# Strassen feed-forward stage: wider weight rings half a product later, combining of the sums spread over the last weight tiles

## The chip, the cores and the metric

The kernel runs on one core of a Trainium2 chip. The metric is device time in microseconds (us); the kernel before took 2602.29 us, the median of three runs (2601.42 to 2602.42). The profile is of one further execution of the same program.

## The reference, cut to what matters

One decoder layer on 512 tokens of width 2048, all in float32: a mixing half (two groups of recurrent heads, an output projection, norms), and then the feed-forward (FF) half, which is where the change lies:

```python
h = rmsnorm(x, pre_ffn_norm[l]) * (1.0 + sc_f) + sh_f
y = jnp.square(jax.nn.relu(h @ w_ff1[l])) @ w_ff2[l]      # 2048 -> 8192 -> 2048
x = x + gt_f * rmsnorm(y, post_ffn_norm[l])
```

## The kernel before

**Split products.** Each float32 matrix is split into a rounded part (H) and a remainder (L), and a product is three matmuls: H by H, L by H and H by L. For the weights this is done on the fly by `WeightStream`: SyncE (SP) loads a 128x1024 tile into `raw`, ScalarE (ACT) casts it to `wh` (line 197), VectorE (DVE) subtracts to get `wl` (line 199). I call this subtraction the split.

**The order of the weights** is a plan, a list of tiles numbered from 0, which `get` hands out one by one. With each `get` it also issues loads, casts and splits of some tiles further on. Tiles 168 to 171 are the first four of the FF stage, 504 and 505 the last two of the first FF matrix, 506 to 509 and 510 to 513 the eight after them.

**The rings.** `raw`, `wh` and `wl` are rings of 3, 2 and 2 buffers in the pool `wpool`, which lives through the whole kernel. In the FF stage `ws.wide` is set to the pool `fp`, and then every second `raw` and every third `wh`/`wl` comes from `fp` instead (tags `raw2`, `wh2`, `wl2`), so that the rings are twice and one and a half times as deep; `get` also works two tiles ahead instead of one. `fp` takes the memory that the stage in between (pool `mid`) had, so a tile of `fp` can only be written once the last instruction on `mid` is done.

**The stage in between** ends with 16 blocks of `h2`, the input of the FF stage: for each, TensorE (PE) transposes (line 1519), DVE scales (line 1525), ACT makes `h2H` (line 1528, or lines 1533 and 1534 for every third block), and DVE (line 1529) or, for every third block, GpSimd (POOL, line 1535) makes `h2L`. The last two blocks are number 14 (its `h2L` on POOL) and 15 (on DVE). The first FF product runs between these transposes.

**The FF stage.** The 8192 hidden units go in 16 rounds of 512. `ff1(r, g)` makes half a round: 4 weight tiles (q = 0 to 3), 24 matmuls each, 96 in all; tile q needs the `h2` blocks 4q to 4q+3. `ff2s(r, m)` multiplies into the second matrix by Strassen's seven products (84 matmuls), whose results DVE adds onto `y2` and, for products 4 and 5, onto `m45`. Only after the last of these can `gather` combine `m45` and the quarters of `y2`: 24 additions of 128x512 on DVE, line 1634. The last round is not by Strassen: its halves of the second matrix (`ff2_mm`, banks `pg`, at the end `pl`) are multiplied plainly. The order before the end is `ff2s(14, 1)`, `plain(0)`, `gather`, `ff1(15, 1)`, `plain(1)`, then the plain products. Two weight tiles of these (510 and 511) are written as `walt` into the memory of `m45`.

**What sets the order.** In the FF loop PE and SP run in the order in which the code calls them; on DVE, ACT and POOL a scheduler orders the instructions when the program is built. Behind that, each engine takes its instructions strictly in turn, and SP starts its transfers in turn.

Of the kernel before, what the change touches and what calls it, by code (L numbers as in the profile page):

```python
# [13 lines left out]
ALU = mybir.AluOpType  # L14
# [221 lines left out]
def hybrid_layer_kernel(  # L236
# [7 lines left out]
    nc = tc.nc  # L244
# [63 lines left out]
    def ff_order():  # L308

        yield from ((1, 0, 0), (1, 0, 1))  # L310
        for r in range(NR - 1):
            last = r == NR - 2
            yield from ((1, r + 1, 0), (2, r, 0))
            yield from ((2, r, 1), (1, r + 1, 1)) if last else ((1, r + 1, 1), (2, r, 1))
# [30 lines left out]
    ws = WeightStream(nc, wpool, plan, 3, 1, (3, 2, 2))  # L345
# [119 lines left out]
    def mm3(ps, aH, aL, bH, bL, start, stop):  # L465
        mm(ps, aH, bH, start, False)
        mm(ps, aH, bL, False, False)
        mm(ps, aL, bH, False, stop)
# [436 lines left out]
    def pj(name):  # L905
        return bank("pj", name)
# [538 lines left out]
    with ExitStack() as st:  # L1445
# [70 lines left out]
        for kt in range(KT):  # L1516
# [10 lines left out]
            if kt % 3 < 2:  # L1527
                nc.scalar.activation(out=h2H[:, kt, :], in_=ht, func=AF.Identity, bias=shf[:, kt : kt + 1])
                nc.vector.scalar_tensor_tensor(out=h2L[:, kt, :], in0=ht, scalar=shf[:, kt : kt + 1],
                                               in1=h2H[:, kt, :].bitcast(F32), op0=ALU.add, op1=ALU.subtract)  # L1530
            else:
# [4 lines left out]
                                        op=ALU.subtract)  # L1536
# [3 lines left out]
    with ExitStack() as st:  # L1540
        fp = st.enter_context(tc.tile_pool(name="ff", bufs=1))
        y2 = big.tile([P, 4, D], F32, tag="y", name="y2")
# [14 lines left out]

        m45 = fp.tile([P, 4, 1024], F32, tag="m45", name="m45")
        gs, cs_, gHL = {}, {}, []

        def ff1(r, g):
            if g == 0:
                gs[r] = fp.tile([P, 2, 2, T], F32, tag="g", name=f"g{r}")
            col = r * RB * P + g * 256
            pss_ = [pj(f"pf{col}_{cb}") for cb in range(2)]
            for q in range(4):
                wH, wL = ws.get(("f1", col, q))
                for cb in range(2):
                    for kk in range(4):
                        kt = q * 4 + kk  # L1570
                        cs = slice(cb * P, (cb + 1) * P)
                        mm3(pss_[cb], wH[:, kk, cs], wL[:, kk, cs], h2H[:, kt, :], h2L[:, kt, :],
                            kt == 0, kt == KT - 1)
            for cb in range(2):
                v = gs[r][:, cb, g, :]
                nc.scalar.activation(out=v, in_=pss_[cb], func=AF.Relu)
                nc.scalar.activation(out=v, in_=v, func=AF.Square)

        def combos(r):

            cH = fp.tile([P, 2, 7, 256], F32R, tag="cH", name=f"cH{r}")
            cL = fp.tile([P, 2, 7, 256], F32R, tag="cL", name=f"cL{r}")
            for jj in range(2):
                S = fp.tile([P, 5, 256], F32, tag="gS", name=f"gS{r}_{jj}")
                g4 = gs[r][:, jj].rearrange("p h (t n) -> p (h t) n", t=2)
                nc.vector.tensor_tensor(out=S[:, 0:2, :], in0=g4[:, 0:2, :], in1=g4[:, 2:4, :], op=ALU.add)
                nc.vector.tensor_tensor(out=S[:, 2:4, :], in0=g4[:, 1:3, :], in1=g4[:, 0::3, :], op=ALU.subtract)
                nc.vector.tensor_tensor(out=S[:, 4, :], in0=g4[:, 0, :], in1=g4[:, 3, :], op=ALU.add)
                nc.scalar.copy(out=cH[:, jj, 0:5, :], in_=S)
                nc.vector.tensor_tensor(out=cL[:, jj, 0:5, :], in0=S, in1=cH[:, jj, 0:5, :].bitcast(F32),  # L1590
                                        op=ALU.subtract)
                nc.scalar.copy(out=cH[:, jj, 5:7, :], in_=g4[:, 0::3, :])
                nc.vector.tensor_tensor(out=cL[:, jj, 5:7, :], in0=g4[:, 0::3, :],
                                        in1=cH[:, jj, 5:7, :].bitcast(F32), op=ALU.subtract)
            cs_[r] = (cH, cL)
# [13 lines left out]
        def ff2s(r, m):  # L1609
            cH, cL = cs_[r]  # L1610
            for i, *_ in SEVEN:
                wH, wL = ws.get(("s2", r, m, i))
                for tb in range(2):
                    ps = bank(RING[nps[0] % 5], f"pg{r}_{m}_{i}_{tb}")
                    nps[0] += 1
                    ts = slice(tb * P, (tb + 1) * P)
                    for jj in range(2):
                        mm3(ps, cH[:, jj, PLACE[i], ts], cL[:, jj, PLACE[i], ts], wH[:, jj, :], wL[:, jj, :],
                            jj == 0, jj == 1)
                    for dst, first in sums_of(i, m, tb):  # L1620
                        if r == 0 and first:
                            nc.vector.tensor_copy(out=dst, in_=ps)
                        else:
                            nc.vector.tensor_tensor(out=dst, in0=ps, in1=dst, op=ALU.add)  # L1624

        def gather(m):

            lo_, hi_ = slice(m * 512, (m + 1) * 512), slice(1024 + m * 512, 1024 + (m + 1) * 512)
            for tb in range(2):
                c11, c12, c21, c22 = y2[:, tb, lo_], y2[:, tb, hi_], y2[:, 2 + tb, lo_], y2[:, 2 + tb, hi_]  # L1630
                m4, m5 = m45[:, tb, lo_], m45[:, 2 + tb, lo_]
                for dst, v, op in ((c11, m4, ALU.add), (c11, m5, ALU.subtract), (c22, c12, ALU.add),
                                   (c22, c21, ALU.subtract), (c12, m5, ALU.add), (c21, m4, ALU.add)):
                    nc.vector.tensor_tensor(out=dst, in0=dst, in1=v, op=op)  # L1634

        def plain(g):

            r = NR - 1
            if g == 0:
                gHL.append(fp.tile([P, RB, T], F32R, tag="cH", name="gH"))  # L1640
                gHL.append(fp.tile([P, RB, T], F32R, tag="cL", name="gL"))
            for cb in range(2):
                j = 2 * g + cb
                nc.scalar.copy(out=gHL[0][:, j, :], in_=gs[r][:, cb, g, :])
                nc.vector.tensor_tensor(out=gHL[1][:, j, :], in0=gs[r][:, cb, g, :],
                                        in1=gHL[0][:, j, :].bitcast(F32), op=ALU.subtract)
# [26 lines left out]
                next(steps, None)  # L1673

        ws.on_get = on_get
        ws.wide = fp
        ws.nraw, ws.ring = 0, []
        with tc.manual_schedule(engines={ET.PE, ET.SP}):
            for kind, r, g in ff_order():
                if kind == 1:  # L1680
                    ff1(r, g)
                    if g == 1 and r == 0:
                        combos(0)
                    if r == NR - 1 and g == 1:
                        plain(1)
                else:
                    ff2s(r, g)
                    if g == 1 and r < NR - 2:
                        combos(r + 1)
                    elif g == 1:  # L1690
                        plain(0)
                        gather(0)
                        gather(1)
            for _ in steps:
                pass

# [99 lines left out]
```

## Time and profile before

| what | value |
|---|---|
| median of three runs | 2602.29 us |
| the profiled execution: its time, its span from first to last instruction | 2601.19 us, 2599.4 us |
| PE busy | 2476.1 us, 95% |
| DVE busy | 1876.1 us, 72% |
| ACT busy | 1119.0 us, 43% |
| POOL busy | 1034.3 us, 40% |
| chain that ended last: PE, DVE | 66%, 6% of the span |
| FF stage | from about 1245.6 us to the end |

PE is busy nearly all the time, so what counts are the places where it is not. These are found in the chain that ended last (which engine carried the time in each stretch), and then in the timeline of PE, where a bracket behind a row gives the idle time before it and what ended it. Times in such rows are from the start of the span.

### The profile page before, as it was taken

What the parts mean: (1) busy time and instruction counts of PE and PEld (TensorE: products, weight loads), DVE (VectorE), ACT (ScalarE), POOL (GpSimd) and SP (SyncE); (2) the same over time, 40 slices, a digit from 0 to 9 for tenths busy, and PEclk for the clock granted to TensorE, in tenths of its full rate; (3) what the DMA queues carried; (4) which work ended last, traced back from release to release, by engine and by line L of the source; (5) the groups of instructions that cost most, each with busy time, mean ns of one, the idle gap of its engine ahead of it and who ended that gap; (6) DMA issues with size and microseconds to landing.
All of it is one profiled execution on the core that took longest, in us unless ns stands there. A gap on an engine that the chain in (4) does not pass through costs nothing.

```text
span 2599.4 us, 34113 instructions
## 1 busy us (share of the span) xinstructions
PE 2476.1 (95%) x12627; PEld 2008.6 (77%) x12627; DVE 1876.1 (72%) x2709; ACT 1119.0 (43%) x1765; POOL 1034.3 (40%) x646
## 2 busy tenths in 40 slices
PE   5889999998999899999899999999999999999998
PEld 3667777777877788788688888888888888888876
DVE  7997877767676675634568776787767877677696
ACT  5543544444444442423444444444444444434333
POOL 5561344445454540000144535445354453533423
PEclk9999999999999999999899999999999999999999
DMA  9762434444544432435323333333324334233234
GB/s 324 253 196 78 131 120 139 139 155 139 156 151 142 154 107 90 140 128 170 122 98 135 101 134 105 134 131 105 134 97 142 130 100 140 85 122 109 89 113 160
DMA packets 127300, 350.64 MB, mean 135 GB/s; under 512 B 14247, under 2 KB 18713, under 8 KB 125981
## 3 DMA queue, kind: packets, MB, share of 16 engines
q1 hardware_dynamic: 126938, 348.41, 40.0%
q8 instruction: 99, 1.62, 0.3%
q14 instruction: 67, 0.55, 0.1%
q10 hardware_dynamic: 196, 0.06, 0.0%
HBM read 340.01 MB, written 8.40 MB: 134 GB/s over the span
## 4 chain that ended last, share of the span: by engine, by line
PE 66%; DVE 6%; POOL 1%; ACT 1%; issue 1%; DMA 1%; SPq 0%; DVEq 0%; ACTq 0%; POOLq 0%
PE pf L331 26%; PE pg L331 21%; PE pj L331 9%; PE pout L331 7%; DVE wl L199 1%; PE pa L331 1%; DMA ada<-in_w_ada_dram 1%; DVE y L1634 0%; POOL y L1720 0%; DVE y L1624 0%; DVE uc L1034 0%; POOL aacc L451 0%; DVE utmp L1032 0%; DVE x2r L1738 0%; PE p L331 0%
## 5 line engine op out<-in xcount | busy, mean ns | idle before, releaser
L199 DVE TENSOR_TENSOR wl<-raw,wh 128x1024 fp32r<-128x1024 f32 x506 | 723.9, 1432 | 441.8 <-ACT wh L197 438.5
L197 ACT CAST wh<-raw 128x1024 fp32r<-128x1024 f32 x512 | 538.2, 1052 | 946.3 <-PE pf L331 286.0
L165 POOL TENSOR_TENSOR raw<-raw,raw 128x1024 f32<-128x1024 f32 x150 | 439.9, 2948 | 401.6 <-DMA raw<-in_w_ff_dram 154.0
L331 PE MATMUL pf<-h2H,wh 128*128 128x512 f32 x1024 | 401.3, 392 | 6.6 <-ACT wh L197 6.6
L331 PE MATMUL pf<-h2H,wl 128*128 128x512 f32 x1024 | 401.1, 392 | 4.5 <-DVE wl L199 4.4
L331 PE MATMUL pf<-h2L,wh 128*128 128x512 f32 x1024 | 400.9, 391 | 0.0
L451 POOL TENSOR_TENSOR aacc<-ada,aacc 128x512 f32<-128x512 f32 x180 | 270.7, 1504 | 254.5 <-ACT ada L449 243.2
L331 PE MATMUL pg<-wl,cH 128*128 128x512 f32 x840 | 327.4, 390 | 1.1 <-DVE wl L199 1.0
L331 PE MATMUL pg<-wh,cL 128*128 128x512 f32 x840 | 326.8, 389 | 0.0
L331 PE MATMUL pg<-wh,cH 128*128 128x512 f32 x840 | 326.8, 389 | 0.0
L331 PE MATMUL pj<-hH,wh 128*128 128x512 f32 x768 | 325.3, 424 | 0.0
L331 PE MATMUL pj<-hH,wl 128*128 128x512 f32 x768 | 305.2, 397 | 4.3 <-DVE wl L199 4.3
L331 PE MATMUL pj<-hL,wh 128*128 128x512 f32 x768 | 304.0, 396 | 0.0
L331 PEld LDWEIGHTS pf<-h2H,wh 128*128 128x128 f32 x1024 | 193.7, 189 | 47.1 <-ACT wh L197 7.0
L331 PEld LDWEIGHTS pf<-h2H,wl 128*128 128x128 f32 x1024 | 193.5, 189 | 45.7 <-DVE wl L199 5.6
L331 PEld LDWEIGHTS pf<-h2L,wh 128*128 128x128 f32 x1024 | 193.6, 189 | 40.2
L451 POOL TENSOR_TENSOR gacc<-ada,gacc 128x512 f32<-128x512 f32 x64 | 108.5, 1695 | 277.9 <-ACT ada L449 277.9
L1624 DVE TENSOR_TENSOR y<-pg,y 128x512 f32<-128x512 f32 x344 | 218.9, 681 | 0.0
L331 PEld LDWEIGHTS pg<-wl,cH 128*128 128x128 f32 x840 | 157.6, 188 | 35.7 <-DVE wl L199 3.1
L331 PEld LDWEIGHTS pg<-wh,cH 128*128 128x128 f32 x840 | 157.7, 188 | 32.9
L331 PEld LDWEIGHTS pg<-wh,cL 128*128 128x128 f32 x840 | 157.7, 188 | 32.6
L331 PEld LDWEIGHTS pj<-hH,wl 128*128 128x128 f32 x768 | 146.5, 191 | 39.6 <-DVE wl L199 6.5
(434 smaller groups left out, 3762.2 us busy)
## 6 DMA issues: line engine op xcount, KB each, us to landing
raw<-in_w_ff_dram SPq DMA_DIRECT2D x256, 512.0 KB, 4.0
raw<-in_w_in_dram SPq DMA_DIRECT2D x128, 512.0 KB, 3.4
ada<-in_w_ada_dram SPq DMA_DIRECT2D x256, 256.0 KB, 3.5
adas<-in_w_ada_dram SPq DMA_DIRECT2D x128, 256.0 KB, 4.3
raw<-in_w_out_dram SPq DMA_DIRECT2D x40, 512.0 KB, 3.5
xo<-in_x_dram SPq DMA_DIRECT2D x8, 512.0 KB, 9.7
xr<-in_x_dram SPq DMA_DIRECT2D x8, 512.0 KB, 6.3
x2d<-z SPq DMA_DIRECT2D x4, 1024.0 KB, 3.9
```

The lines of the kernel that those rows point to most:

```text
L165: self.nc.gpsimd.tensor_tensor(out=out, in0=ra, in1=rb, op=op)
L197: self.cast = self.nc.scalar.copy(out=h, in_=raw).ins
L199: eng.tensor_tensor(out=lo, in0=raw, in1=h.bitcast(F32), op=ALU.subtract)
L331: nc.tensor.matmul(ps, lhsT=lhsT, rhs=rhs, start=start, stop=stop)
L451: nc.gpsimd.tensor_tensor(out=acc, in0=a, in1=acc, op=ALU.add)
L1624: nc.vector.tensor_tensor(out=dst, in0=ps, in1=dst, op=ALU.add)
```

## The change

Two edits, both in the FF stage.

First, `ws.wide = fp` (and the reset of the raw ring) is no longer set ahead of the FF loop but behind the first `ff1`, after four weight tiles. Tiles 168 to 171 thus stay in `wpool`'s rings of 3, 2 and 2, with `get` working one tile ahead for the split and three for the loads.

Second, `gather` becomes a generator that issues one addition per step and holds the additions in program order. It is no longer run in one piece before `ff1(15, 1)`: each of that function's four weight tiles takes five steps right behind its `get`, and what is left (four) comes behind `ff1(15, 1)`. The 24 additions are the same, on the same operands.

```diff
@@ ff1
                 wH, wL = ws.get(("f1", col, q))
+                for _ in range(5):
+                    next(joins, None)
                 for cb in range(2):
@@ gather
-        def gather(m):
...
-            for tb in range(2):
...
-                    nc.vector.tensor_tensor(out=dst, in0=dst, in1=v, op=op)
+        def gather():
+            for m in range(2):
...
+                for tb in range(2):
...
+                        tc.keep_in_program_order(nc.vector.tensor_tensor(out=dst, in0=dst, in1=v, op=op))
+                        yield
@@ the FF loop
         ws.on_get = on_get
-        ws.wide = fp
-        ws.nraw, ws.ring = 0, []
         with tc.manual_schedule(engines={ET.PE, ET.SP}):
             for kind, r, g in ff_order():
                 if kind == 1:
                     ff1(r, g)
+                    if (r, g) == (0, 0):
+
+                        ws.wide = fp
+                        ws.nraw, ws.ring = 0, []
                     if g == 1 and r == 0:
                         combos(0)
                     if r == NR - 1 and g == 1:
+                        for _ in joins:
+                            pass
                         plain(1)
                 else:
                     ff2s(r, g)
...
                     elif g == 1:
                         plain(0)
-                        gather(0)
-                        gather(1)
+                        joins = gather()
```

What stands on DVE at the start of the FF stage, where tiles 170 and 171 (the third and fourth of the first product) are split, before:

```order
L1525 SCALAR_TENSOR_TENSOR h2t14_11407<-pm14_11402,sc1f_102,R_10324 128x512
L1525 SCALAR_TENSOR_TENSOR h2t15_11418<-pm15_11413,sc1f_102,R_10324 128x512
L1529 SCALAR_TENSOR_TENSOR h2L_11272<-h2t15_11418,shf_103,h2H_11271 128x512
L199 TENSOR_TENSOR wl170_11441<-raw170_11052,wh170_11440 128x1024
L199 TENSOR_TENSOR wl172_11501<-raw1_11474,wh172_11500 128x1024
L199 TENSOR_TENSOR wl173_11531<-raw2_11504,wh173_11530 128x1024
```

and now:

```order
L1525 SCALAR_TENSOR_TENSOR h2t14_11407<-pm14_11402,sc1f_102,R_10324 128x512
L1525 SCALAR_TENSOR_TENSOR h2t15_11418<-pm15_11413,sc1f_102,R_10324 128x512
L199 TENSOR_TENSOR wl171_11499<-raw171_11436,wh171_11498 128x1024
L1529 SCALAR_TENSOR_TENSOR h2L_11272<-h2t15_11418,shf_103,h2H_11271 128x512
L199 TENSOR_TENSOR wl172_11529<-raw172_11466,wh172_11528 128x1024
L199 TENSOR_TENSOR wl174_11571<-raw174_11526,wh174_11570 128x1024
```

Before, the split of 170 stood behind the last `h2L`, and that of 171 twelve rows above it, between the scalings of blocks 9 and 10. Now 170 stands in that higher place and 171 just ahead of the last `h2L`.

The SP queue in the same place, before:

```order
L1468 DMA xr3_1_11247<-in_x_dram 128x1024
L1483 DMA x2d_10315<-z_10319 128x2048 x2
L140 DMA raw1_11474<-in_w_ff1_dram 128x1024
L140 DMA raw2_11504<-in_w_ff1_dram 128x1024
L140 DMA raw3_11534<-in_w_ff1_dram 128x1024
```

and now:

```order
L1468 DMA xr3_1_11247<-in_x_dram 128x1024
L1483 DMA x2d_10315<-z_10319 128x2048 x2
L140 DMA raw173_11496<-in_w_ff1_dram 128x1024
L140 DMA raw174_11526<-in_w_ff1_dram 128x1024
L1546 DMA gacc2_11429<-in_b_ada_dram 1x2048
L431 DMA ada5_0_0_11534<-in_w_ada_dram 128x512
L140 DMA raw0_11574<-in_w_ff1_dram 128x1024
L140 DMA raw1_11604<-in_w_ff1_dram 128x1024
```

`raw1` of before (tile 172) was the first tile of `fp` in this queue. Now tiles 173 and 174 go into `wpool`, 172 is loaded before the rows shown, and the first load into `fp` is `raw1` of now (tile 176).

DVE around the combining, before (the end of it, with the splits of tiles 504 to 507):

```order
L1634 TENSOR_TENSOR y2_11428<-y2_11428,m45_11430 128x512 x3
L1634 TENSOR_TENSOR y2_11428<-y2_11428 128x512
L199 TENSOR_TENSOR wl504_20630<-raw303_20517,wh504_20629 128x1024
L1634 TENSOR_TENSOR y2_11428<-y2_11428 128x512
L1634 TENSOR_TENSOR y2_11428<-y2_11428,m45_11430 128x512 x2
L199 TENSOR_TENSOR wl505_20660<-raw304_20633,wh505_20659 128x1024
L199 TENSOR_TENSOR wl506_20690<-raw305_20663,wh506_20689 128x1024
L199 TENSOR_TENSOR walt_20794<-raw309_20833,walt_20794 128x1024
L199 TENSOR_TENSOR wl507_20720<-raw306_20693,wh507_20719 128x1024
```

and now, from the last sum of Strassen's products on:

```order
L1627 TENSOR_TENSOR m45_11430<-pg14_1_5_1_20589,m45_11430 128x512
L1650 TENSOR_TENSOR gL_20598<-g15_20156,gH_20597 128x512 x2
L199 TENSOR_TENSOR wl504_20606<-raw299_20517,wh504_20605 128x1024
L1638 TENSOR_TENSOR y2_11428<-y2_11428,m45_11430 128x512 x2
L1638 TENSOR_TENSOR y2_11428<-y2_11428 128x512 x2
L1638 TENSOR_TENSOR y2_11428<-y2_11428,m45_11430 128x512
L199 TENSOR_TENSOR wl505_20641<-raw300_20609,wh505_20640 128x1024
L1638 TENSOR_TENSOR y2_11428<-y2_11428,m45_11430 128x512 x3
L1638 TENSOR_TENSOR y2_11428<-y2_11428 128x512 x2
L199 TENSOR_TENSOR wl506_20676<-raw301_20644,wh506_20675 128x1024
L1638 TENSOR_TENSOR y2_11428<-y2_11428,m45_11430 128x512 x4
L1638 TENSOR_TENSOR y2_11428<-y2_11428 128x512
```

The split of 504 stood behind 21 of the 24 additions (one of them stood earlier, amid the last Strassen products) and now stands ahead of all 24; then come five additions per split, and the `walt` splits have moved behind the splits of 507, 508 and 509.

## Rows read from the trace of the kernel before

**Rows 1.** The chain that ended last, merged: start us, us, what.

```profile
1272.27 55.40 PE pf L331 x238
1327.66 19.04 PE pg L331 x84
1346.70 21.76 PE pf L331 x96
```

**Rows 2.** Timeline of PE, start of the FF stage: start us, us, instruction.

```profile
1263.99 0.39 PE L331 MATMUL pf<-h2H,wl 128*128 128x512 f32 x1
1271.01 0.80 PE L331 MATMUL pf<-h2H,wh 128*128 128x512 f32 x1 [6.62 <-ACT wh L197]
...
1274.89 0.39 PE L331 MATMUL pf<-h2H,wl 128*128 128x512 f32 x1
```

**Rows 3.** Waits of the DMA queue SP, 1230 to 1330: total us, times, longest.

```profile
SPq L140 <- DVE h2L L1529: 29.3, 1, 29.3
```

**Rows 4.** Timeline of DVE, start of the FF stage.

```profile
1265.74 1.40 DVE L1525 SCALAR_TENSOR_TENSOR h2t<-pm,sc1f,R 128x512 f32<-128x512 f32 x2
1268.60 1.23 DVE L1529 SCALAR_TENSOR_TENSOR h2L<-h2t,shf,h2H 128x512 fp32r<-128x512 f32 x1 [1.47 <-ACT h2H L1528]
```

**Rows 5.** Timeline of ACT, start of the FF stage.

```profile
1256.73 1.06 ACT L197 CAST wh<-raw 128x1024 fp32r<-128x1024 f32 x1 [1.84 <-PE pf L331]
...
1263.32 1.38 ACT L1528 ACTIVATE h2H<-h2t,shf 128x512 fp32r<-128x512 f32 x2
1266.57 0.72 ACT L1533 ACTIVATE h2s<-h2t,shf 128x512 f32<-128x512 f32 x1 [1.88 <-DVE h2t L1525]
...
1269.91 1.04 ACT L197 CAST wh<-raw 128x1024 fp32r<-128x1024 f32 x1 [1.34 <-POOL h2L L1535]
```

**Rows 6.** Timeline of POOL, start of the FF stage.

```profile
1268.02 1.26 POOL L1535 TENSOR_TENSOR h2L<-h2s,h2H 128x512 fp32r<-128x512 f32 x1 [3.41 <-ACT h2H L1534]
```

**Rows 7.** Page, part 6, DMA issues: count, KB each, median us to landing.

```profile
raw<-in_w_ff_dram SPq DMA_DIRECT2D x256, 512.0 KB, 4.0
```

**Rows 8.** Timeline of PE, end of the FF stage.

```profile
2507.43 0.39 PE L331 MATMUL pg<-wh,cH 128*128 128x512 f32 x1
2507.92 0.50 PE L331 MATMUL pg<-wl,cH 128*128 128x512 f32 x1
...
2510.57 0.39 PE L331 MATMUL pf<-h2H,wh 128*128 128x512 f32 x1
...
2521.67 0.39 PE L331 MATMUL pf<-h2L,wh 128*128 128x512 f32 x1
2522.52 1.19 PE L331 MATMUL pg<-wh,gH 128*128 128x512 f32 x4 [0.46 <-ACT wh L197]
2528.16 0.80 PE L331 MATMUL pf<-h2H,wl 128*128 128x512 f32 x1 [4.45 <-DVE wl L199]
...
2541.36 0.39 PE L331 MATMUL pf<-h2H,wl 128*128 128x512 f32 x1
...
2564.74 0.62 PE L331 MATMUL pl<-walt,gH 128*128 128x512 f32 x2
```

**Rows 9.** Timeline of DVE, end of the FF stage.

```profile
2489.77 2.61 DVE L199 TENSOR_TENSOR wl<-raw,wh 128x1024 fp32r<-128x1024 f32 x1
...
2500.20 0.67 DVE L1634 TENSOR_TENSOR y<-y,m 128x512 f32<-128x512 f32 x1
...
2514.85 0.67 DVE L1634 TENSOR_TENSOR y<-y,m 128x512 f32<-128x512 f32 x1
...
2526.89 1.21 DVE L199 TENSOR_TENSOR wl<-raw,wh 128x1024 fp32r<-128x1024 f32 x1
```

**Rows 10.** Timeline of ACT, end of the FF stage.

```profile
2521.42 1.05 ACT L197 CAST wh<-raw 128x1024 fp32r<-128x1024 f32 x1 [4.38 <-PE pf L331]
```

**Rows 11.** Timeline of POOL, end of the FF stage.

```profile
2488.90 9.09 POOL L165 TENSOR_TENSOR raw<-raw,raw 128x1024 f32<-128x1024 f32 x3 [1.33 <-DMA raw<-in_w_ff_dram]
```

**Rows 12.** One window: us, then busy us (count) of PE, PEld, DVE, ACT, POOL; PEclk.

```profile
2500.00:2545.00 45.00, 39.99 (x161) 31.54 (x160) 38.22 (x53) 15.05 (x18) 0.00 (x0) 0.92 0.42 132
```

More of the change, by code (lines that the diff above doesn't have):

```diff
@@ L1559, in hybrid_layer_kernel @@
         gs, cs_, gHL = {}, {}, []
+        joins = iter(())
         def ff1(r, g):
@@ L1624, in ff2s @@
                             nc.vector.tensor_tensor(out=dst, in0=ps, in1=dst, op=ALU.add)
-        def gather(m):
-            lo_, hi_ = slice(m * 512, (m + 1) * 512), slice(1024 + m * 512, 1024 + (m + 1) * 512)
-            for tb in range(2):
[L1630 to L1633, printed above, removed]
-                    nc.vector.tensor_tensor(out=dst, in0=dst, in1=v, op=op)
+        def gather():
+            for m in range(2):
+                lo_, hi_ = slice(m * 512, (m + 1) * 512), slice(1024 + m * 512, 1024 + (m + 1) * 512)
+                for tb in range(2):
+                    c11, c12, c21, c22 = y2[:, tb, lo_], y2[:, tb, hi_], y2[:, 2 + tb, lo_], y2[:, 2 + tb, hi_]
+                    m4, m5 = m45[:, tb, lo_], m45[:, 2 + tb, lo_]
+                    for dst, v, op in ((c11, m4, ALU.add), (c11, m5, ALU.subtract), (c22, c12, ALU.add),
+                                       (c22, c21, ALU.subtract), (c12, m5, ALU.add), (c21, m4, ALU.add)):
+                        tc.keep_in_program_order(nc.vector.tensor_tensor(out=dst, in0=dst, in1=v, op=op))
+                        yield
         def plain(g):
```

## The prediction

> **What bounds the kernel now.** I read the chain that ended last first, in order of time. In the FF stage it lies on PE: 96 matmuls of a first-matrix product take 21.76 us and the 84 of a Strassen group 19.04 us [rows 1], 0.2267 us each, round after round. Nothing that spares DVE, ACT or DMA there is worth anything; only time in which PE doesn't run counts. The timeline of PE shows two such stretches, one at each end of the FF stage, and the edits lie on them. The reader is to see, in each, which instruction PE waits for, and what that one stood behind.
>
> At the start, PE is through the first two weight tiles with the matmul at 1263.99 and starts the third tile, 170, only at 1271.01, released by ACT's cast [rows 2]. That cast starts at 1269.91 [rows 5], right after the last h2L, which runs from 1268.60 for 1.23 us to 1269.83 [rows 4]. The data had been there: what held the cast is its buffer, the first of `fp`, which opens when `mid` is finished. SP's queue says the same: a weight load stood 29.3 us until that h2L [rows 3].
>
> At the end, PE runs through the last first-matrix product from 2510.57 [rows 8]. It multiplies with wh of tile 504 up to 2521.67, squeezes in 4 matmuls of the next product, and resumes at 2528.16, released by the split of 504. That split stands at 2526.89 [rows 9], behind 20 additions which began at 2514.85: (2526.89 - 2514.85)/20 = 0.60 us each.
>
> **The change part by part.**
>
> *A, the rings half a product later.* PE would go on at 1263.99 + 0.23 = 1264.22. It restarts at 1271.01: 6.79 us. Then the 8 matmuls before 1274.89 take 3.88 us [rows 2] where 8 x 0.2267 = 1.81 do at full clock: another 2.07 us at the lower of the two clock levels, 1.2 instead of 2.4 GHz, after that idle stretch. Together 8.86 us, if nothing else is late.
>
> What is late next? Tile 170 now takes the place that 171 had on ACT and DVE, and that one was cast at 1256.73 [rows 5], so with its split (1.2) it is ready by 1259.1. Tile 171 needs wh's second buffer, free when PE ends the second tile at about 1264.4. Its cast stands on ACT between the instruction that ends at 1263.32 + 1.38 = 1264.70 and the one at 1266.57, before which ACT sat idle 1.88 us for DVE [rows 5]. A cast of 1.06 fits, 1264.70 to 1265.76. Its split stands on DVE behind the two scalings that end at 1265.74 + 1.40 = 1267.14, and DVE then idled 1.47 us [rows 4], in which 1.21 fits. So neither delays h2. PE reaches tile 171 at 1264.22 + 24 x 0.2267 = 1269.66; it wants block 14 six matmuls later, at 1271.0, and block 15 at 1271.7. They are there by 1268.02 + 1.26 = 1269.28 [rows 6] and 1269.83.
>
> One rule speaks against this hiding. The last h2L took 1.23 us beside POOL's h2L of 1268.02, with 1.26 us [rows 4, 6]. The Trainium skill, "SBUF — State Buffer", section "Who interferes with whom", says that a VectorE instruction with two SBUF inputs and a GpSimd instruction that reads SBUF exclude each other, whichever comes second waiting for the whole of the other. By it the inserted split, until 1268.35, would hold POOL's h2L for 0.33 us and the last h2L until about 1270.4; the sum would stay as it is, and the chance that A loses a little is larger for it. The trace agrees in kind.
>
> The next product: 172 is loaded early now and takes the wh buffer of 170 at 1269.7, so it is ready by 1272.2, wanted at 1275.1. 174 waits for raw 171's buffer (1268.4), a transfer of 4.0 us [rows 7], cast and split: 1274.7. 173 takes the wh buffer of 171, free at 1275.3: ready at 1277.7, wanted at 1280.5. The loads of `fp` come behind `mid`'s end at 1269.83 for tiles wanted after 1290. So I take A at -8.86. The other end: the cast and split of 171 push the last h2L back by their whole 1.06 + 1.21 = 2.27 us, to 1272.1, where PE wants it at 1271.7; 0.4 us would go, and -8.4 be left. A longer wait there is among the rivals.
>
> *B, the additions spread.* From 2521.67 + 0.23 = 2521.90 to the last matmul of the product, 2541.36 + 0.23 = 2541.59, 19.69 us pass. In them run 96 - 50 = 46 matmuls of the product (50 lie between 2510.57 and 2521.67, (11.10/0.2267) + 1) and the 4 of the next [rows 8]: 50 x 0.2267 = 11.34. Lost: 8.35 us, again idle time and a stretch of matmuls at the lower clock behind it (the mean granted clock is 0.92 between 2500 and 2545 [rows 12]).
>
> Now the split of 504 stands ahead of all additions: where these began, at about 2514.3 to 2515.5, for a use at 2521.9. Then each weight tile brings five additions and one split, 5 x 0.60 + 1.21 = 4.2 us of DVE, beside 24 x 0.2267 = 5.44 us of PE. The cast of 506 comes at 2521.42, released by PE [rows 10]; its split ends by 2524 and is wanted at 2532. 507 is ready by 2529.2, wanted at 2537.7. The last four additions and the two gL splits end near 2536. So B is -8.35.
>
> *C, one addition less before.* One addition ran at 2500.20 [rows 9] amid the last Strassen group, where DVE had no gap, and PE loses 2507.92 - 2507.43 - 0.23 = 0.26 and some tenths about it [rows 8]. The addition gone, DVE is 0.60 us ahead. Between 0 and -0.6; I take -0.4.
>
> *D, what the additions hold.* The two casts of `walt` wait for the end of the additions, as m45 gives them its memory, and now stand on ACT among the casts of gacc2 behind the product, on which PE waits a little. Two casts are 2 x 1.06: cost between 0 and 2.1, below nothing not, since they leave no place that PE waited on. PE has the 20 matmuls of the next product ahead of that, 4.5 us, so I take +0.4. Their real use is the matmul at 2564.74 [rows 8], some 8 us earlier now, 2556; they are split by 2546.
>
> Both edits change no instruction count that matters: the same 24 additions, casts, splits and loads. The end behind the last product moves along with PE.
>
> Sum: -8.86 - 8.35 - 0.4 + 0.4 = -17.2. The profiled execution took 2601.19 us, its span 2599.4 and 1.8 around it; it would take 2584.0. The median of the runs stands 1.1 above it, so I predict 2602.29 - 17.2 = 2585.1.
>
> **The rivals.**
>
> *One half is lost.* Either h2 or a late tile holds PE at the start, or the additions hold the splits at the end. For the latter each DVE instruction would have to slow as one split did beside POOL's additions, 2.61 us against 1.21 [rows 9, 11]: +1.4 on six instructions is 8.4, so 12.6 against PE's 5.44 per tile, a new stall worth all of B. That is the rule named above, taken to the end. Against it: POOL is busy 0.00 us between 2500 and 2545 [rows 12]. With B gone the time is 2602.29 - 8.9 = 2593.4; with A gone, 2593.9; with half of either, about 2589 to 2590.
>
> *Neither comes.* PE's waits turn out to be followed by others of the same length, at h2 and at the tail, where DVE's and POOL's work behind the last matmul could set the end whenever PE is through. Against it: the additions and casts there stand in PE's order and move along. 2600 to 2603.
>
> *Slower: the phase of the rings.* The count that picks every third wh from `fp` now starts four tiles later, so each of the 15 Strassen rounds meets the ring one tile out of step with before. If one tile per round then came late by cast and split, 1.06 + 1.21 = 2.27 us, the price is 15 x 2.27 = 34 us, and the time 2602.3 + 34 - 17.2 = 2619. From 17.2/15 = 1.15 us per round on it decides. Against it: a round takes 22 tiles, no multiple of three, so before already ran through all phases, with the same 21.76 and 19.04 us.
>
> **How the numbers follow.** Both halves as worked out: 0.77, with its own range 2583 to 2588 (C and D at their ends, small losses of A). One half lost, wholly or partly: 0.13, 2589 to 2594. Neither: 0.05. Slower: 0.05. The range runs from 2581.5, for some waits of PE amid the last Strassen group that go too, to 2594. A measurement of this kernel tells about 0.2%, 5.2 us, from no change. Faster by more 0.90, within 0.05, slower by more 0.05.
>
> **What would show it.** A right: PE's row at 1271.01 loses its bracket, tile 170's matmuls start near 1264.2 at 0.39 us each, and the chain's PE stretch of 238 matmuls starts earlier by 8 to 9 us against the last transpose. B right: no PE idle time above 0.5 us between the last Strassen product and the first matmul on `walt`, granted clock 1.00 there, and the splits of 504 to 507 five additions apart. A wrong if PE waits behind 1264 for h2L or a split; B wrong if PE waits on line 199 in that product. The forecast as a whole is wrong if the rounds between are no longer 40.80 us.

## The result and the profile after

| | before | after |
|---|---|---|
| median of six runs | 2602.36 us (2601.42 to 2603.99) | 2585.27 us (2582.80 to 2589.01) |
| ratio, 95% interval | | 0.9934 [0.9921, 0.9947] |
| profiled execution, its span | 2601.19, 2599.4 us | 2583.66, 2581.9 us |

The change takes 17.1 us by the medians and 17.5 us by the two spans; 17.2 were forecast. To see where they went, the FF stage is cut at six matmuls of PE's timeline, each given by its start:

| us on PE | before | after | difference |
|---|---|---|---|
| last matmul of tile 169 | 1263.99 | 1264.31 | +0.32, drift ahead of the FF stage |
| from it to the first Strassen matmul | 63.51 | 54.63 | -8.88 |
| 28 pairs of a Strassen group and a product, 40.80 each | 1142.40 | 1142.40 | 0 |
| the last two Strassen groups, 168 matmuls with no product between them (to the last first-matrix product) | 40.67 | 40.12 | -0.55 |
| from there to the first matmul on `walt` | 54.17 | 45.77 | -8.40 |
| from there to the last matmul | 21.53 | 21.53 | 0 |

Below, the stretches are called the start (63.51 us before), the last groups (40.67) and the end (54.17).

**The start.** The chain of waits of the changed kernel, answering to [rows 1]: start us, us, what.

```profile
1262.86 56.24 PE pf L331 x248
1319.10 19.04 PE pg L331 x84
1338.14 21.76 PE pf L331 x96
```

Where the chain began a stretch of 238 matmuls at 1272.27, it now runs over 248 without a break. The PE timeline, answering to [rows 2]:

```profile
1264.31 0.39 PE L331 MATMUL pf<-h2H,wl 128*128 128x512 f32 x1
1264.54 0.39 PE L331 MATMUL pf<-h2H,wh 128*128 128x512 f32 x1
```

The second row is the first matmul of tile 170: no bracket, 0.39 us in place of 0.80. SP's waits from 1236 to 1330, answering to [rows 3]:

```profile
SPq L140 <- DVE wl L199: 77.1, 10, 18.4
```

No load waits for an h2L any more; the 77.1 us are loads that wait for a raw buffer until a split has read it. None of them held PE, which runs through here. And DVE, answering to [rows 4], then POOL, answering to [rows 6]:

```profile
1267.39 1.21 DVE L199 TENSOR_TENSOR wl<-raw,wh 128x1024 fp32r<-128x1024 f32 x1
1268.93 1.37 DVE L1529 SCALAR_TENSOR_TENSOR h2L<-h2t,shf,h2H 128x512 fp32r<-128x512 f32 x1 [0.34 <-ACT h2H L1528]
```

```profile
1268.35 1.40 POOL L1535 TENSOR_TENSOR h2L<-h2s,h2H 128x512 fp32r<-128x512 f32 x1 [3.42 <-ACT h2H L1534]
```

The split of 171 lies in the gap that DVE had there. POOL's h2L beside it takes 1.40 us in place of 1.26, and the last h2L ends at 1268.93 + 1.37 = 1270.30; PE, which wants it at about 1272.0, doesn't wait.

**The end.** PE's timeline, answering to [rows 8]:

```profile
2501.46 0.39 PE L331 MATMUL pf<-h2H,wh 128*128 128x512 f32 x1
...
2523.00 0.39 PE L331 MATMUL pf<-h2H,wl 128*128 128x512 f32 x1
...
2547.23 0.62 PE L331 MATMUL pl<-walt,gH 128*128 128x512 f32 x2
```

The last first-matrix product takes 21.54 us from the start of its first matmul to that of its last, where it took 30.79. DVE beside it, answering to [rows 9]:

```profile
2505.74 1.21 DVE L199 TENSOR_TENSOR wl<-raw,wh 128x1024 fp32r<-128x1024 f32 x1
2506.87 1.41 DVE L1638 TENSOR_TENSOR y<-y,m 128x512 f32<-128x512 f32 x2
2508.19 1.41 DVE L1638 TENSOR_TENSOR y<-y 128x512 f32<-128x512 f32 x2
2509.52 0.69 DVE L1638 TENSOR_TENSOR y<-y,m 128x512 f32<-128x512 f32 x1
2510.12 1.22 DVE L199 TENSOR_TENSOR wl<-raw,wh 128x1024 fp32r<-128x1024 f32 x1
```

From one split to the next, with five additions between, 2510.12 - 2505.74 = 4.38 us pass (forecast 4.2), under PE's 5.44. The window that answers to [rows 12] (PE, PEld, DVE, ACT, POOL busy; PEclk 1.00):

```profile
2500.00:2545.00 45.00, 45.00 (x199) 36.71 (x198) 42.63 (x58) 17.80 (x25) 1.29 (x1) 1.00 0.54 198
```

ACT behind the product, where the forecast put its term D (`g` is the product's activated output, `gH` and `gL` its two parts; `gf` is the same for `gacc`, the gate of the FF output, which PE sums into `pgf`):

```profile
2525.44 0.62 ACT L1649 CAST gH<-g 128x512 fp32r<-128x512 f32 x1
2526.25 1.06 ACT L197 CAST walt<-raw 128x1024 fp32r<-128x1024 f32 x1 [0.19 <-DVE y L1638]
2527.21 1.13 ACT L460 CAST gf<-gacc 128x512 fp32r<-128x512 f32 x2
2528.25 1.04 ACT L197 CAST walt<-raw 128x1024 fp32r<-128x1024 f32 x1
```

The first `walt` cast waits 0.19 us for the last addition and stands behind the last gH. PE has no idle time of note there.

### The profile page after: what moved, and what is told of

It is laid out like the page before. It is cut to its first block, busy times and chain, and to the rows that moved or that the text cites. A ratio compares the mean times of both kernels' runs of the same rounds, so it can differ in the third digit from the quotient of the medians.

```text
span 2581.9 us, 34110 instructions
## 1 busy us (share of the span) xinstructions
PE 2469.1 (96%) x12627; PEld 2007.2 (78%) x12627; DVE 1875.9 (73%) x2709; ACT 1118.1 (43%) x1765; POOL 1032.4 (40%) x646
## 4 chain that ended last, share of the span: by engine, by line
PE 67%; DVE 6%; POOL 1%; ACT 1%; issue 1%; DMA 1%; DVEq 0%; ACTq 0%; POOLq 0%
PE pf L331 27%; PE pg L331 22%; PE pj L331 9%; PE pout L331 7%; DVE wl L199 1%; DVE uc L1034 1%; PE pa L331 1%; DVE utmp L1032 1%; POOL y L1728 0%; POOL aacc L451 0%; PE p L331 0%; DVE x2r L1746 0%; DMA ada<-in_w_ada_dram 0%; DVE zkT L493 0%; PE pz L331 0%
```

## The experiments

The times are medians; the kernel before stood at 2603.34, 2603.51 and 2605.00 us in the three groups in which they ran (nearly all runs of one kernel lie within 4 to 6 us there, and the ratios have intervals of about ±0.12%). The three stretches in the trace repeat far better, and the verdicts rest on them:

| run | start | last groups | end | median | ratio to before |
|---|---|---|---|---|---|
| before | 63.51 | 40.67 | 54.17 | | |
| changed kernel again | 54.63 | 39.93 | 45.73 | 2585.25 | 0.9926 [0.9914, 0.9939] |
| rings alone | 54.63 | 40.67 | 53.40 | 2594.74 | 0.9970 [0.9958, 0.9982] |
| additions alone | 63.47 | 39.92 | 45.75 | 2594.81 | 0.9971 [0.9959, 0.9983] |
| phase of wh | 56.96 | 40.74 | 53.82 | 2597.21 | 0.9975 [0.9966, 0.9984] |
| PE kept busy | 62.42 | 40.43 | 52.03 | 2600.40 | 0.9991 [0.9981, 1.0000] |
| additions at the first tile | 54.63 | 40.46 | 47.52 | 2589.10 | 0.9942 [0.9930, 0.9955] |
| additions behind | 54.63 | 39.77 | 55.73 | 2596.03 | 0.9971 [0.9960, 0.9982] |
| POOL beside | 54.63 | 39.89 | 62.99 | 2604.23 | 0.9999 [0.9990, 1.0008] |
| kept, at the old place | 54.63 | 40.08 | 46.52 | 2587.75 | 0.9937 [0.9923, 0.9950] |
| spread, not kept | 54.63 | 40.52 | 47.58 | 2588.73 | 0.9940 [0.9927, 0.9954] |
| two products on DVE | 54.63 | 39.99 | 45.77 | 2585.20 | 0.9928 [0.9915, 0.9940] |
| tail scaling split | 54.63 | 39.99 | 45.76 | 2585.08 | 0.9925 [0.9913, 0.9938] |

**The rings alone.**

```diff
-        ws.wide = fp
-        ws.nraw, ws.ring = 0, []
...
                     ff1(r, g)
+                    if (r, g) == (0, 0):
+                        ws.wide = fp
+                        ws.nraw, ws.ring = 0, []
```

> The kernel before with the first edit alone: the wide rings come into use behind the first half product; the 24 additions stand in one piece where they stood. Theory (two separate stretches of PE, each worth its own sum): the start gives back 8.9 us and the end nothing, so 2602.3 - 8.9 = 2593.4; the first Strassen matmul, 1327.66 before, starts near 1318.8, and between the matmul that ended wh of tile 504 and the split of 504 PE still stands idle some 6 us. Rival (the two gains hang together, as what is gained early is given back where the next buffer is waited for): 2600 or more, or the whole 2585.

Measured: 8.6 us less by the medians, -8.88 at the start. The end keeps its stall and is only 0.77 us shorter, in PE's timeline:

```profile
2514.21 0.39 PE L331 MATMUL pf<-h2L,wh 128*128 128x512 f32 x1
2515.05 1.21 PE L331 MATMUL pg<-wh,gH 128*128 128x512 f32 x4 [0.46 <-ACT wh L197]
2520.72 0.79 PE L331 MATMUL pf<-h2H,wl 128*128 128x512 f32 x1 [4.45 <-DVE wl L199]
```

The bracket is the 4.45 us of [rows 8], and nothing gained at the start was given back before it. The 0.77 us lie behind the bracket, where fewer matmuls are slow (10 in place of 14).

**The additions alone.** The changed kernel, with the rings back at their old place.

```diff
+        ws.wide = fp
+        ws.nraw, ws.ring = 0, []
         with tc.manual_schedule(engines={ET.PE, ET.SP}):
...
-                    if (r, g) == (0, 0):
-                        ws.wide = fp
-                        ws.nraw, ws.ring = 0, []
```

> The changed kernel with the first edit taken back: rings as before, additions spread by five. Theory: the end gives back 8.3 us and the addition amid the last Strassen group some 0.5, so 2602.3 - 8.8 = 2593.5; PE still idles 6.8 us ahead of tile 170 (1264.2 to 1271.0), and the last first-matrix product takes 21.5 to 21.8 us from its start to its last matmul in place of 30.8. Rival (the additions merely move the wait to the next split): 2600 or more.

Measured: -8.5 us by the medians. In PE's timeline the wait at the start is as it was:

```profile
1273.97 0.79 PE L331 MATMUL pf<-h2H,wh 128*128 128x512 f32 x1 [6.64 <-ACT wh L197]
```

The two halves add up: 8.6 and 8.5 us by the medians, 17.1 for both. In the traces the rings give -8.88 at the start, the additions -0.75 in the last groups and -8.42 at the end, and both together -17.83, so each stretch answers to its own edit. The theory of two separate stretches stands.

**The phase of wh.** Which of the two waits at the start was the hold, the buffer or the load?

```diff
         ws.wide = fp
         ws.nraw, ws.ring = 0, []
+        ws.nw = 2
```

> The kernel before with one number changed: the count that picks every third wh from the wide pool starts at 2 in place of 0, so that tile 170 keeps its wh in the narrow pool and tile 171 is the first with its wh in the wide one. The raw loads still go to the wide pool at the old place, behind the last h2L in SP's queue. Theory (the hold is the one wh buffer of tile 170): PE runs on through tile 170 from 1264.2, wants tile 171 at 1269.7, its cast can start at 1269.9 and its split ends at about 1272.2: some 1.3 us of wait for the cast and as much again for the split, so 6 to 7.5 of the 8.9 us come back, 2594.8 to 2596.3. Rival (the hold is the weight load that stands 29.3 us in SP's queue): nothing or little comes back, or PE waits as long one or two tiles later, 2600 to 2602.3.

Measured: 6.55 us of the 8.88 come back. PE's timeline has two short waits, one tile later:

```profile
1274.72 0.50 PE L331 MATMUL pf<-h2H,wh 128*128 128x512 f32 x1 [1.22 <-ACT wh L197]
...
1275.98 0.50 PE L331 MATMUL pf<-h2H,wl 128*128 128x512 f32 x1 [0.53 <-DVE wl L199]
```

The load in SP's queue still stands there, as long as before [rows 3]:

```profile
SPq L140 <- DVE h2L L1529: 29.0, 1, 29.0
```

So the hold was the one wh buffer of tile 170; the load held nothing that PE wanted soon. The matmuls behind waits of 1.22 and 0.53 us run at full clock (granted clock 1.00 from 1270 to 1290). The median, 2597.21, lies 0.9 us above the expected range; the kernel before stood 1.0 higher in this group than the expectation took it.

**PE kept busy.** The kernel before, with matmuls in both idle stretches whose result is not used.

```diff
+                if q == 2 and (r, g) in ((0, 0), (NR - 1, 1)):
+                    spare = bank("wh" if r == 0 else "sh", f"spare{r}")
+                    for _ in range(28 if r == 0 else 20):
+                        nc.tensor.matmul(spare, lhsT=onesr, rhs=h2H[:, 0, :], start=True, stop=True)
```

> The kernel before, with matmuls added whose result nobody reads: 28 (128x512) in the idle stretch ahead of tile 170 and 20 in the one ahead of the split of 504. Both waits stay as they are; only PE's idling goes. Theory (behind an idle stretch the matmuls run at the lower clock, and that is part of each loss): PE resumes at full clock, so 2.1 us come back at the start and 3.0 at the end (8.35 less the idle stretch), 2602.3 - 5 = 2597.3, with a granted clock of 1.00 in both stretches. Rival (the slow matmuls behind the wait are slow since operands or DMA are late, not by the clock): 2602, the matmuls behind the wait as slow as before.

Measured: -2.9 us by the medians, with an interval that just reaches no change, so the stretches carry the reading: the start gives back 1.09 and the end 2.14, of 2.1 and 3.0 expected. PE's timeline at the start:

```profile
1267.65 6.51 PE L1571 MATMUL spare<-h2H,onesr 128*128 128x512 f32 x28
1274.50 0.50 PE L331 MATMUL pf<-h2H,wh 128*128 128x512 f32 x1 [0.34 <-ACT wh L197]
1274.84 0.40 PE L331 MATMUL pf<-h2L,wh 128*128 128x512 f32 x1
1275.77 0.50 PE L331 MATMUL pf<-h2H,wl 128*128 128x512 f32 x1 [0.53 <-DVE wl L199]
```

No matmul is slow behind the wait, and the granted clock is 1.00. One window of the kernel before, then of this one (us, then PE, PEld, DVE, ACT, POOL busy; PEclk):

```profile
1264.00:1284.00 20.00, 13.34 (x51) 10.13 (x50) 7.96 (x8) 7.08 (x11) 3.68 (x3) 0.83 0.64 236
```

```profile
1264.00:1284.00 20.00, 19.13 (x86) 15.03 (x84) 11.26 (x13) 8.04 (x11) 4.41 (x3) 1.00 0.47 183
```

So the slow matmuls were slow by the clock and not by late operands. But a fast PE meets the next wait: the split of 170 takes 1.23 us behind its cast, and 0.53 us of idling take the place of slow matmuls that had covered it. Part of the "clock" in term A was thus a second wait in hiding. At the end the granted clock is 1.00 too, from 2500 to 2545; there 0.7 us go to three matmuls of the next product that no longer fit ahead of the split.

**All additions at the first tile.** The changed kernel, 24 steps at q = 0 and the order left to the scheduler.

```diff
-                for _ in range(5):
+                for _ in range(24 if q == 0 else 0):
...
-                        tc.keep_in_program_order(nc.vector.tensor_tensor(out=dst, in0=dst, in1=v, op=op))
+                        nc.vector.tensor_tensor(out=dst, in0=dst, in1=v, op=op)
```

> The changed kernel with the additions not spread: all 24 stand behind the get of the first weight tile of the last product, in an order left to the scheduler, by which DVE's row is split of 504, 21 additions, split of 505, 3 additions, 506, 507. Theory (PE waits for whatever split stands behind more additions than fit beside the tiles ahead): the split of 504 ends near 2507, 21 x 0.60 = 12.6 us of additions follow, the split of 505 ends at about 2520.8, and PE wants it one tile later than 504's, near 2512.6: some 6 to 8 us of stall and slow matmuls if the additions start at 2507; less, 3 to 5, as PE may squeeze in other matmuls. So 2585.3 + 4 to 8 = 2589 to 2593. Rival (only the first split counts, as the tiles behind it have slack): 2585.

Measured: a miss in size. The median, 2589.10, does lie at the lower edge of the expected range, but that is luck: the end grew by 1.75 us and not by 4 to 8, and the rest is spread among runs and an addition that the scheduler put amid the last groups (+0.3), which the expectation didn't have there. The timelines of DVE and of PE:

```profile
2521.07 0.68 DVE L1638 TENSOR_TENSOR y<-y 128x512 f32<-128x512 f32 x1
2521.67 1.21 DVE L199 TENSOR_TENSOR wl<-raw,wh 128x1024 fp32r<-128x1024 f32 x1
```

```profile
2520.96 0.61 PE L331 MATMUL pg<-wh,gH 128*128 128x512 f32 x2
2522.93 0.50 PE L331 MATMUL pf<-h2H,wl 128*128 128x512 f32 x1 [1.36 <-DVE wl L199]
```

The mechanism is the one expected, PE waits for the split of 505 behind the block of additions. The size isn't: tile 505 is the fourth of the product, so its split is wanted 3 x 5.44 + 0.45 = 16.8 us after the start at 2504.19, at 2521.0, and comes at 2522.8. The end is 47.52 us. The expectation had put the tile's use one tile and more too early.

**All additions behind the product.** The changed kernel without the steps in `ff1`.

```diff
-                for _ in range(5):
+                for _ in range(0):
```

> The changed kernel with no addition in the last product: all 24 stand behind its splits and gL, ahead of what the last second-matrix products need. Theory (the additions cost nothing only where a weight tile gives PE 5.44 us): the four splits come early, but the splits for the products behind, and walt that lies in m45's memory, come behind 24 x 0.60 = 14.5 us of additions; PE wants the first of them near 2528 and gets it 5 to 9 us late, 2590 to 2595. Rival (the place of the additions is free as long as the four splits stand ahead of them): 2585.

Measured: +10 us at the end, more than term B and more than the 5 to 9 expected; the time, 2596.03, is above the expected range. PE's timeline:

```profile
2543.07 1.40 PE L331 MATMUL pgf<-gf,onesr 128*128 128x512 f32 x2 [2.92 <-DVE gf L461]
2548.12 0.79 PE L331 MATMUL pg<-wh,gH 128*128 128x512 f32 x1 [3.65 <-DVE y L1670]
```

The four splits are early and the product runs through in 21.76 us. The waits, 2.92 + 3.65 us with matmuls at a granted clock of 0.50 behind them (2543 to 2552), have moved to gf and to the sums that free PE's banks, which queue on DVE behind and between the additions. That the splits come first is thus not enough: the 24 x 0.60 = 14.4 us of additions must also lie beside the product, in the slack that DVE has between the splits.

**POOL beside.** The forecast's first rival, made to happen.

```diff
+                if (r, g) == (NR - 1, 1):
+                    if q == 0:
+                        S7 = fp.tile([P, 5, 256], F32, tag="gS", name="S7")
+                    for _ in range(4 if q < 3 else 2):
+                        nc.gpsimd.tensor_tensor(out=S7[:, 0:2, :].rearrange("p a n -> p (a n)"),
+                                                in0=y2[:, 0, 0:512], in1=y2[:, 2, 1024:1536], op=ALU.add)
```

> The changed kernel with 14 additions more on POOL (128x512, both inputs in SBUF, result unused) in the stretch of the last first-matrix product, where POOL had 0.00 us of work. They test the forecast's first rival, by which DVE and POOL hold each other up. If the price per DVE instruction is that of the split beside POOL's additions, 2.61 us against 1.21, a weight tile's six DVE instructions take up to 12.6 us beside PE's 5.44, as long as POOL's row lasts (14 x 1.2 = 17 us or more), and PE would wait 4 to 10 us: 2589 to 2595. If the price is small for additions of 0.60 us, the tile stays under 5.44 and the time at 2585 to 2586. My theory: DVE slows by about a half while POOL runs, 4.2 to some 6.5 per tile, which the slack of 5 us ahead of the second split takes in: 2585 to 2588.

Measured: a miss. All of the change's gain is gone, +17.2 us at the end, more than any theory gave. DVE, POOL, ACT and PE, a timeline each:

```profile
2514.45 2.32 DVE L199 TENSOR_TENSOR wl<-raw,wh 128x1024 fp32r<-128x1024 f32 x1
2516.69 5.18 DVE L1644 TENSOR_TENSOR y<-y,m 128x512 f32<-128x512 f32 x3
```

```profile
2514.01 25.26 POOL L1575 TENSOR_TENSOR S<-y 128x512 f32<-128x512 f32 x14 [20.21 <-DVE y L1644]
```

```profile
2545.39 1.04 ACT L197 CAST walt<-raw 128x1024 fp32r<-128x1024 f32 x1 [15.07 <-DVE y L1644]
2546.35 1.13 ACT L460 CAST gf<-gacc 128x512 fp32r<-128x512 f32 x2
```

```profile
2547.01 0.79 PE L331 MATMUL pgf<-gf,onesr 128*128 128x512 f32 x1 [14.80 <-ACT gf L460]
```

From start to start, a DVE addition takes (2521.79 - 2516.69)/3 = 1.70 us in place of 0.60 and a split 2516.69 - 2514.45 = 2.24 in place of 1.13: each pays 1.1 us, whatever its own length. Beside POOL's fourteen additions stand just fourteen DVE instructions, eleven additions and three splits; and eleven of POOL's last 1.6 to 1.7 us and three 2.1 to 2.2, longer by what a split takes over an addition (1.13 - 0.60). So the two engines take turns, one instruction for one, and each pays the other's time too. The Trainium skill, "SBUF — State Buffer", section "Who interferes with whom", states this exclusion for a VectorE instruction with two SBUF inputs beside a GpSimd instruction that reads SBUF, and the trace agrees.

A tile then took 10.7 us of DVE (2514.45 to the split at 2525.19), and still PE's product ran without a break: the split of 504 stood ahead of the crowd, and that of 505 (2514.45) ended 5.7 us before its use at 2505.73 + 3 x 5.44 + 0.45 = 2522.5. The loss came behind the product, where the last additions ended at 2545.4. PE wanted gf, and ACT's cast to gf stood behind the `walt` cast, which waited 15.07 us for the additions. But gf lies in the memory of g, which the second gL reads, and gL, on DVE amid the additions, ended only at 2545.28 + 0.68 = 2545.96. Without the `walt` cast gf could have started some 0.4 us earlier, so nearly all of the loss is DVE's lateness and not ACT's order.

**Kept order, at the old place.** In the changed kernel, the generator is run through at the place where `gather` was called.

```diff
-                        joins = gather()
+                        for _ in gather():
+                            pass
```

> The changed kernel with the 24 additions issued in one piece at their old place, but each kept in program order as in the change. The scheduler then builds, of itself, DVE's row as 1 addition, split of 504, 6 additions, split of 505, 6, split of 506, 6, split of 507, 5. Theory (what counts is how many additions stand ahead of each split on DVE, 6 x 0.60 + 1.21 = 4.8 us a tile being under PE's 5.44, and not the code that puts them there): 2585 to 2586.5, with no idle time of PE in the product. Rival (the additions have to be tied to the tiles by hand): 2590 or more.

Measured: the end takes 46.52 us, 0.75 more than in the changed kernel; the product has no idle time, and DVE's row is the one expected. The median, 2587.75, is 1.25 us above the expected range; the trace shows no more than the 0.75. The scheduler, bound only by the kept order, spreads the additions by itself, and nearly all of B comes.

**Spread, not kept.**

```diff
-                        tc.keep_in_program_order(nc.vector.tensor_tensor(out=dst, in0=dst, in1=v, op=op))
+                        nc.vector.tensor_tensor(out=dst, in0=dst, in1=v, op=op)
```

> The changed kernel with the additions issued five behind each weight tile, but not kept in program order; the scheduler then puts them on DVE as split of 504, 5, split of 505, 7, split of 506, 7, split of 507, with none amid the last Strassen group. Theory (only the number of additions ahead of each split counts, and seven of them with a split, 7 x 0.60 + 1.21 = 5.4 us, are just as long as PE's 24 matmuls): the same as the changed kernel within 0.5 us in the trace. Rival (the kept order itself matters): 2 us or more slower.

Measured: a miss, +1.8 us at the end and +0.4 in the last groups. One addition does stand amid the last Strassen group, against the expectation. The timelines of ACT and of PE show the rest:

```profile
2528.73 1.05 ACT L197 CAST walt<-raw 128x1024 fp32r<-128x1024 f32 x1 [1.76 <-DVE y L1638]
2529.68 0.59 ACT L1579 ACTIVATE g<-pf 128x512 f32<-128x512 f32 x1
...
2531.64 1.04 ACT L197 CAST walt<-raw 128x1024 fp32r<-128x1024 f32 x1
2532.58 0.62 ACT L1649 CAST gH<-g 128x512 fp32r<-128x512 f32 x1
2534.57 1.14 ACT L460 CAST gf<-gacc 128x512 fp32r<-128x512 f32 x2 [1.37 <-DVE gL L1650]
```

```profile
2535.24 0.50 PE L331 MATMUL pgf<-gf,onesr 128*128 128x512 f32 x1 [1.39 <-ACT gf L460]
```

The product runs through, but here the `walt` casts stand ahead of g and gH. They hold ACT 1.76 us for the last addition and then for their own two casts; so gH is late, gL behind it, and gf, which waits for gL, comes to PE 1.39 us late. This is the forecast's term D with its price. The kept order by itself doesn't spare it: in the run before this one, which has that order, the `walt` casts stand ahead of the second gH as well, the first of them waiting 0.65 us, and its end is 0.75 us longer. In the changed kernel they stand behind the last gH; what made the scheduler place them there was not tested.

**The tail.** Two more runs looked for a faster version: two of eight multiplications moved from POOL to DVE (the first hunk), and then also a block's scaling split between ACT and DVE (the second).

```diff
-                weigh(tok, nb, nc.gpsimd)
+                weigh(tok, nb, nc.vector if (tok, nb) in ((1, 1), (3, 1)) else nc.gpsimd)
...
-            if (tok, i) == (3, 1):
+            if (tok, i) in ((0, 1), (1, 1), (2, 1), (3, 1)):
                 nc.scalar.activation(out=yv, in_=yv, func=AF.Copy, scale=rs)
-                nc.gpsimd.tensor_tensor(out=xr[:, tok, cs], in0=yv, in1=xr[:, tok, cs], op=ALU.add)
+                (nc.gpsimd if tok == 3 else nc.vector).tensor_tensor(out=xr[:, tok, cs], in0=yv, in1=xr[:, tok, cs], op=ALU.add)
```

> The changed kernel with two of the eight multiplications by the norm's weight, which run on POOL as one row of 10.5 us in the tail, done on DVE. The chain of waits of the changed kernel runs over that row and then over DVE, whose first scaling starts at 2556.85, behind POOL's small step that ends the row. Theory: that scaling starts 0.9 us earlier and the end moves along, -0.8 us in the trace (tail from the last matmul to the end 12.3 in place of 13.1 us). Rival (the end hangs on the last matmul alone): the tail stays at 13.1.

> As the run before, and the second half of each token block's scaling is split: ACT multiplies by the norm's factor, DVE only adds (1.13 us by the splits' rows, which have the same form, in place of 1.75). Theory (DVE's row is what sets the tail once POOL's is shorter): another 0.6 us for each of two or three blocks, the tail at 11 to 11.7 us, 1.4 to 2 us under the changed kernel. Rival (ACT's result comes late and DVE waits for it): no more than the run before, or longer.

Measured: from the last matmul to the end of the span, 2581.9 - 2568.76 = 13.14 us pass in the changed kernel, 2580.6 - 2568.14 = 12.46 in the first of these and 2583.4 - 2570.87 = 12.53 in the second. The first gain is 0.7 us, of 0.8 expected; the second gives nothing more, where 11 to 11.7 us had been expected for the tail. The timelines of DVE and of POOL in the second show why:

```profile
2566.71 1.70 DVE L1744 TENSOR_TENSOR x2r<-y,x2r 128x1024 f32<-128x1024 f32 x1 [0.54 <-ACT y L1743]
...
2575.24 1.23 DVE L1744 TENSOR_TENSOR x2r<-y,x2r 128x1024 f32<-128x1024 f32 x1 [0.56 <-ACT y L1743]
```

```profile
2565.71 1.62 POOL L1728 TENSOR_TENSOR y<-y,Gf 128x512 f32<-128x512 f32 x1 [0.86 <-ACT tail L1727]
```

DVE waits for ACT, and the plain addition takes 1.23 us alone and 1.70 beside POOL. The scaling that it replaced takes no longer by itself: the 1.75 us of the expectation are the mean of two in one row of the changed kernel, one of 1.28 and this one, which began while a POOL multiplication ran:

```profile
2558.06 2.31 DVE L1746 SCALAR_TENSOR_TENSOR x2r<-y,rsf,x2r 128x1024 f32<-128x1024 f32 x1
```

Neither is told from the changed kernel by its time.

**The changed kernel again.**

> The changed kernel itself, on the chip of the experiments, as the measure for them: 0.9934 times the kernel before, 2586 where that takes 2603.4. In its trace the stretches have the lengths of the first trace of it (54.6 us from the last matmul of tile 169 to the first Strassen matmul, 45.8 us from the start of the last first-matrix product to the first matmul on walt) whatever the drift ahead of them.

Measured: 2585.25 us, and the stretches within 0.2 us of the first trace.

## Why the prediction was right

Its time was 0.2 us off the median. That close a hit is partly chance, since runs of one kernel spread over 5 us; the terms are the better test.

- **A, -8.86: right, -8.88**, in every run that has the edit. The place named as the hold, tile 170's wh buffer, was confirmed by the phase of wh, and the later buffers were ready as worked out. By the exclusion rule that the forecast named, the last h2L would end at about 1270.4 and by the sum at 1269.83; it ended at 1270.30, of which 0.32 are drift. So it was pushed back by 0.15 us where the rule gave some 0.6, and PE had slack for it. The split of the sum into idle time and clock was less exact: with PE kept busy, 1.09 of the 2.07 us came back, the rest being a wait for the split that lay behind the slow matmuls.
- **B, -8.35: right, -8.34**: the product's 30.79 us became 21.54, of which 0.91 are the four matmuls that had been squeezed in and now stand behind it. The tile's 4.2 us of DVE were 4.38.
- **C, -0.4: right in kind, a little more:** -0.55, and -0.74 in the second trace. In the six traces with an addition amid the last groups these take 40.43 to 40.74 us, in the eight without 39.77 to 40.12. The means are 0.6 apart, the forecast's far bound. No run moved this one addition alone, so its part is read from those traces and not tested. Nor is it all that is lost there: 168 x 0.2267 = 38.08 us would do. In the changed kernel PE still waits three times 0.28 to 0.45 us there for a split that takes 2.2 to 2.7 us while POOL sums raw weights, twice its time alone. One such pair, PE's row and DVE's:

```profile
2487.28 0.51 PE L331 MATMUL pg<-wl,cH 128*128 128x512 f32 x1 [0.33 <-DVE wl L199]
```

```profile
2485.00 2.22 DVE L199 TENSOR_TENSOR wl<-raw,wh 128x1024 fp32r<-128x1024 f32 x1
```

- **D, +0.4: mis-sized.** The end shrank by 8.40, so D is 8.34 - 8.40 = -0.06. The casts come behind the last gH and wait 0.19 us. PE had matmuls enough beside the casts. The bound of 2.1 was no idle worry, as the run without kept order paid 1.8 of it with the same additions.
- **The rivals.** "One half lost" was set aside because POOL is idle there; with POOL busy it cost twice what was thought, and by another path: no split held the product, the late additions held gL and gf behind it. "Neither comes" and the phase of the rings are excluded: the 28 pairs between take 1142.40 us in both traces, and in every other.

What no run settled is the drift ahead of the FF stage, up to 5 us between these traces, in a part that no edit touches; it is of the size of the spread among runs of one kernel. Nor did one settle how the scheduler came to ACT's order in the changed kernel, on which D hangs.

## What to carry to other kernels

A wait on PE that a buffer's lifetime causes shows as a bracket behind a cast whose data has long been there; here, moving the switch of the ring by one half product cost the rounds behind it nothing and was worth the whole wait. Work that must be done before a late stage is free only where its engine has slack against the bound engine's tile, so count it tile by tile (4.4 us beside 5.44), and look behind it for an instruction on another in-order engine that waits for its end. Undo each of two edits by itself, and measure stretches between fixed instructions: without a change in them these repeated within 0.4 us, where whole runs differed by 5; a stretch with a stall in it repeated within 0.8.

## What the hardware showed that was not expected

- Behind the same idle stretch of 4.45 us at the end, the slow stretch of matmuls isn't always as long: the product took 31.02 us from its start to the next one's matmuls in the kernel before, 30.27 with the rings alone and 30.68 with the phase of wh; 14, 10 and 13 matmuls were slow. What sets their number no run tells: behind the longer idle stretch at the start, 6.62 us, only 8 were. So up to 0.75 us of a stall's price can't be forecast from one trace. Behind waits of 1.22 to 1.39 us (phase of wh, PE kept busy, additions at the first tile, spread) no matmul was slow.
- DVE and POOL, both adding from SBUF to SBUF, took turns for all of 25 us, one instruction for one, so DVE's additions were slowed nearly threefold (1.70 us against 0.60). The price is the same 1.1 us for a short instruction as for a long one; the forecast had taken 1.4 from a single split.
